# Second layer's first weight group prepared on GpSimd during the first layer's attention

## The chip, the cores and the metric
The kernel runs on one core of a Trainium2 chip. The metric is the time of one execution on the device in microseconds (us), as the median of several runs. The engines are called as in the profile: PE is TensorE's matmuls and PEld its weight loads, DVE is VectorE, ACT is ScalarE, POOL is GpSimd, SP is SyncE. SPq, ACTq and POOLq are the places from which those three issue DMAs.

## What is computed
One inference step of a hybrid encoder with two layers. It runs over a prompt of 2048 tokens and a sample of 32 tokens that share the weights of width 1024. Layer 0 mixes a pooling branch with sliding-window attention; layer 1 is forgetting attention with 16 heads. Each layer is a norm, one combined input projection, a mixer, a gate and an output projection:

```python
def fox_layer(x, k_prefix, v_prefix, logf_prefix, norm_g, w_in, b_forget, qn_g, kn_g, w_out):
    h = rms_norm(x, norm_g)
    proj = h @ w_in
    q, k, v, gate, fpre = jnp.split(proj, [MIX_C, 2 * MIX_C, 3 * MIX_C, 4 * MIX_C], axis=-1)
    ...
    return x + (attn * jax.nn.silu(gate)) @ w_out, k, v, logf
```

All inputs are float32. The kernel gets float32 precision from cheaper matmuls by writing each operand as a sum of two parts, hi (a rounded copy) and lo (the rest), and adding three products: hi with hi, hi with lo, lo with hi.

## The kernel before
The program is one long list of instructions without loops at run time. A planner in the compiler sets the order of the instructions on every engine ahead of the run: where an engine would stand idle by its reckoning, a later instruction that is ready there is put in. During the run each engine, and each queue that issues DMAs, works its list strictly in that order and waits at the head of it.

The stages around the change are these.

- **Layer 0's input projection** (lines 339 to 556) holds the transposed, normalized tokens in `h0` to `h5` of pool `ah`, 16,384 to 24,576 bytes a partition each, with two weight tiles `whl` of 16,384 bytes (pool `aw`) that its column groups use in turn.
- **Layer 0's attention and output projection** (lines 594 to 747) runs in 21 steps over 17 tiles, first the sample and then the 16 tiles of the prompt. A tile goes through five stages, one step each: `stage_load` (L623 to L629: `kk`, `v2` and `qs`, issued from POOL), `stage_scores` (L653 to L665), `stage_values` (L671 to L704, with the gate's product L703 and the split of `mp` on POOL), `stage_out` (L710, and L577 in `out_proj`) and `stage_norm` (L718 to L728). The norm takes its root in `rstd_bits`: L142 to L145 on DVE, then three Newton steps of four small instructions each (L147 to L150) on POOL; then L720 on DVE scales the tile to `hn`, L725 transposes it on PE, L726 copies it out on ACT to `hT`, and L728 stores it to `h1T`. The output weights `wo0` to `wo7` are loaded at step 2 (L564, four of the loads from POOL, four from SP) through the four buffers `xr` and split on ACT and DVE.
- **Layer 1's input projection** (lines 752 to 886) takes `h` back from `h1T` in `load` (L223 into three buffers `hst`, then ACT's cast and DVE's subtraction, L155 and L158 in `split`), and the weights in 16 groups of 256 columns in `weights` (L239 loads 128 rows, L242 scales them by the norm's gains, L155 or L157 and L158 split them into hi and lo). Each group has eight such steps, k = 0 to 7. The first group is prepared by `prefetch` with `fast=True`, on DVE and ACT; every later one on POOL while the group before it is multiplied (L271, or L296 where tokens are the columns). Two tiles `whl` take turns, and three small buffers `wst` take the loads.

SBUF pools are stacked: on the left from the bottom up, on the right from the top down, in the order in which the code opens them. A pool that opens takes the ground of pools that have been closed. An instruction that writes a tile there waits for the last users of the tiles that lay on the same bytes.

Of the kernel before, what the change touches and what calls it, by code (L numbers as in the profile page):

```python
# [17 lines left out]
P = 128  # L18
# [16 lines left out]
CW = 256  # L35
# [7 lines left out]
def hybrid_step_kernel(ctx: ExitStack, tc: tile.TileContext, *args):  # L43
# [93 lines left out]
    def rstd_bits(ss, np_, count):  # L137
        """as rstd_of, for one column and without a table: a first guess from the exponent's bits, then Newton"""
        v = small.tile([P, 1], F32, name="bv", tag="bv")[:np_]
        r = small.tile([P, 1], F32, name="br", tag="br")[:np_]  # L140
        t = small.tile([P, 1], F32, name="bt", tag="bt")[:np_]
        nc.vector.tensor_scalar(out=v, in0=ss, scalar1=1.0 / count, scalar2=EPS, op0=ALU.mult, op1=ALU.add)  # L142
        iv, ir = v.bitcast(I32), r.bitcast(I32)
        nc.vector.tensor_scalar(out=ir, in0=iv, scalar1=1, scalar2=None, op0=ALU.logical_shift_right)
        nc.vector.tensor_scalar(out=ir, in0=ir, scalar1=-1.0, scalar2=float(0x5F3759DF), op0=ALU.mult, op1=ALU.add)  # L145
        for _ in range(3):
            nc.gpsimd.tensor_tensor(out=t, in0=r, in1=r, op=ALU.mult)  # L147
            nc.gpsimd.tensor_tensor(out=t, in0=t, in1=v, op=ALU.mult)
            nc.gpsimd.tensor_scalar(out=t, in0=t, scalar1=-0.5, scalar2=1.5, op0=ALU.mult, op1=ALU.add)
            nc.gpsimd.tensor_tensor(out=r, in0=r, in1=t, op=ALU.mult)  # L150
        return r
# [13 lines left out]
    def flush(n=0):  # L165
        """issue the stores that wait, but for the last n"""
        while len(pending) > n:
            dst, src, eng = pending.pop(0)
            eng.dma_start(dst, src)

    # ------------------------------------------------------------------
    # one layer's input projection, h^T held as exact hi/lo parts
    # ------------------------------------------------------------------
    class Proj:
        def __init__(self, es, w, g, tagp, cw, side):
# [8 lines left out]
            self.wp = es.enter_context(pool_of(name=tagp + "w", bufs=2))  # L184
# [3 lines left out]
        def at(self, which, tok, n):  # L188
            """hi (0) or lo (1) part of h^T for tokens [tok, tok + n): [P, KT, n]"""
# [41 lines left out]
        def weights(self, cols, fast=False):  # L231
            width = sum(n for _, n in cols)
            hl = self.wp.tile([P, 2, KT, self.cw], F32R, name="whl", tag="whl")
            hi, lo = (hl[:, i, :, :width] for i in range(2))
            for k in range(KT):
                st = self.wp.tile([P, self.cw], F32, name="wst", tag="wst", bufs=3)[:, :width]
                at = 0
                for c0, n in cols:
                    nc.sync.dma_start(st[:, at:at + n], self.w[k * P:(k + 1) * P, c0:c0 + n])  # L239
                    at += n  # L240
                eng = nc.vector if fast else nc.gpsimd
                eng.tensor_scalar_mul(st, st, self.g[:, k:k + 1])  # L242
                if fast:
                    split(hi[:, k], lo[:, k], st, nc.scalar, nc.vector)
                else:
                    split(hi[:, k], lo[:, k], st, nc.gpsimd, nc.gpsimd)
            return hi, lo

        def prefetch(self, plan, fast=False):
            """the column groups in the order of use; the next one's weights are loaded ahead"""  # L250
            self.plan = [list(c) for c in plan]
            self.ahead = self.weights(self.plan.pop(0), fast)
# [47 lines left out]
        def turns(self, new=None):  # L300
            """the turn that waits, one step behind the arithmetic it needs"""
# [4 lines left out]
        def head_norm(self, src, np_, nh, gB, eng):  # L306
            """src: [np, nh, 64] (PSUM or SBUF) -> normalized, scaled tile [np, nh, 64]"""
# [13 lines left out]
    def turn(pt, ev, o, t0, h0, npair, dstT):  # L321
        """normalized heads [P, 2 token tiles, npair x 2 heads x 64] -> exact hi / lo parts, transposed"""
# [11 lines left out]
    # ------------------------------------------------------------------  # L334
    # layer 0, input projection and pooling mixer
    # ------------------------------------------------------------------
    smp_es = ExitStack()

    with ExitStack() as es:
# [91 lines left out]
        # ALiBi with the chunk mask, keys = 128 before the tile and its own 128  # L431
# [11 lines left out]
        # the sample's keys, values and queries for the sliding window, hi / lo parts  # L443
# [114 lines left out]
    # ------------------------------------------------------------------  # L558
    # output projection weights, as exact hi/lo parts
    # ------------------------------------------------------------------  # L560
# [6 lines left out]
    def out_proj(pp, pool, lhs, wo, xres, dst, n, eng):  # L567
        """lhs: for 128 tokens (hi, lo) APs [P, KT, 128]; for the sample one AP [P, KT, 64]"""
# [22 lines left out]
    # ------------------------------------------------------------------  # L591
    # layer 0, sliding-window attention and output projection
    # ------------------------------------------------------------------
    with ExitStack() as es:
# [18 lines left out]
        def stage_load(t):  # L613
# [4 lines left out]
            if t < NT:  # L618
# [7 lines left out]
                v2[t] = ld.tile([P, 2, P], F32R, name="v2", tag="v2", bufs=5)  # L626
# [118 lines left out]
        for n in range(NT + 1 + 4):  # L745
            with tc.high_priority(offset=300) if n < 3 else nullcontext():
                step(n)

    # ------------------------------------------------------------------
    # layer 1, input projection  # L750
    # ------------------------------------------------------------------
    late = ctx.enter_context(pool_of(name="late", bufs=1))
    mhs = late.tile([P, KT, 2 * NS], F32R, name="mhs", tag="mhs")
    with ExitStack() as es:
        pj = Proj(es, w_in1, g1c, "c", CW + 16, "right")
# [10 lines left out]
                    + [[(b + c * CW, CW)] for b in (0, 1024, 3072) for c in range(4)], fast=True)  # L766
# [26 lines left out]
        # log forget gates and their running sums  # L793
        with pool_of(name="lf", bufs=1) as lf:
# [28 lines left out]
            def running_sums(src_h, nt, dst, tag):  # L823
                """src_h: [P, 16, nt] with positions t*128+p; dst: DRAM [16*nt, 128]"""
# [63 lines left out]
        # forgetting attention of the sample group, one pair of heads  # L888
# [11 lines left out]
        def sample_pair(hp):  # L900
            """generator: both heads side by side, the queries block diagonal"""
# [70 lines left out]
        for gc in range(4):  # L972
            if gc:
                whi, wlo = pj.next_weights()
            for tch in range(NTC):
                for cc in range(2):
# [3 lines left out]
                    # twice the gate, x * (1 + tanh(x / 2)); the half comes in with the softmax's sums  # L980
# [20 lines left out]
    # ------------------------------------------------------------------  # L1001
    # layer 1, forgetting attention over the prompt
    # ------------------------------------------------------------------
    with ExitStack() as es:
# [9 lines left out]
        def load_head(h, half):  # L1014
            """one head's operands for half of the tokens"""
# [16 lines left out]
        def scores(h, qb, sm, prs):  # L1032
            """generator: one q block's probabilities, in steps"""
# [27 lines left out]
        def values(h, I, prs, dst, a, o):  # L1061
            """generator: one q group's weighted values, transposed, into dst[a]"""
# [53 lines left out]
        def weave(main, n_main, side, n_side):  # L1116
            """side steps spread evenly among the main steps"""
# [66 lines left out]
        # layer 1, output projection  # L1184
# [24 lines left out]
        def halves(t):  # L1209
            """one token tile's mixed values as hi / lo parts"""  # L1210
# [45 lines left out]
```

## Time and profile before
| | us |
|---|---|
| median of 3 runs | 2679.44 |
| lowest and highest | 2678.52, 2679.57 |
| span of the profiled execution, from the first to the last instruction | 2675.6 |

The profile shows one execution on the chip. Its span is 3.8 us below the median of the runs; the rest lies ahead of the first and behind the last instruction. Times of the trace are counted from the start of the span. Matmuls are pipelined, so a busy TensorE is not one at its peak.

### The profile page before, as it was taken

The numbers are of one execution on the slowest core, as the hardware profiler recorded it, in microseconds if no ns is written. First come the engines' busy times: TensorE is split into PE (matmuls) and PEld (weight loads), VectorE is DVE, ScalarE is ACT, GpSimd is POOL, SyncE is SP. The second block draws the span as 40 slices with busy tenths as digits, with TensorE's granted clock in tenths as the row PEclk, the third lists the DMA queues.
The fourth block names the chain that finished last, engine by engine and source line by source line (L and its number), as shares of the span: only waits on it lengthen the run. The fifth ranks groups of instructions, "written<-read, shape, count | busy, mean of one in ns | idle before, by whom it ended". The sixth has DMA issues, their size and how long they took to land. (4 is left out here: it accounts for less than half of the span.)

```text
span 2675.6 us, 47345 instructions
## 1 busy us (share of the span) xinstructions
PE 2586.7 (97%) x17259; PEld 2345.5 (88%) x17259; DVE 1604.6 (60%) x3847; ACT 1166.4 (44%) x2424; POOL 1149.9 (43%) x1583
## 2 busy tenths in 40 slices
PE   6999999799998999999999999999999999999999
PEld 6999999688887999999999998887888878877787
DVE  7650244778765115554553324889988988888521
ACT  5321111556554122222222114777777777777310
POOL 4454240455534434554554422555555555553100
PEclk9999999799998999999999999999999999999999
DMA  6342110976738443445555316544354455443642
GB/s 187 101 110 88 44 47 23 211 185 169 181 100 266 161 159 97 105 111 132 144 146 139 94 62 162 145 113 122 97 148 120 102 120 141 111 103 90 194 149 75
DMA packets 314120, 338.14 MB, mean 126 GB/s; under 512 B 32311, under 2 KB 263887, under 8 KB 313886
## 3 DMA queue, kind: packets, MB, share of 16 engines
q1 hardware_dynamic: 233550, 242.82, 31.6%
q0 software_dynamic: 76320, 87.98, 15.1%
q10 hardware_dynamic: 4016, 4.31, 0.5%
q8 instruction: 136, 2.23, 0.4%
q14 instruction: 98, 0.80, 0.1%
HBM read 203.05 MB, written 132.06 MB: 125 GB/s over the span
## 5 line engine op out<-in xcount | busy, mean ns | idle before, releaser
L271 PE MATMUL pm<-whl,h 128*128 128x256 f32 (+1 forms) x5760 | 713.7, 283 | 6.3 <-ACT h L155 3.1
L271 PEld LDWEIGHTS pm<-whl,h 128*128 128x128 f32 x5760 | 694.9, 190 | 7.9 <-ACT h L155 3.5
L296 PE MATMUL pm<-h,whl 128*128 128x384 f32 (+2 forms) x2880 | 472.3, 322 | 0.0
L296 PEld LDWEIGHTS pm<-h,whl 128*128 128x128 f32 x2880 | 455.3, 188 | 1.8
L158 POOL TENSOR_TENSOR pl<-pf,ph 128x512 fp32r<-128x512 f32 (+3 forms) x270 | 303.6, 1127 | 263.5 <-DVE ph L157 253.2
L1058 ACT ACTIVATE pr<-pr,mnf 128x128 f32<-128x128 f32 (+15 forms) x256 | 309.6, 1211 | 61.6 <-DVE mnf L1053 60.6
L1077 PE MATMUL pt<-ident,pr 128*128 128x128 f32 x2176 | 323.3, 274 | 5.5 <-DVE pl L158 5.4
L1077 PEld LDWEIGHTS pt<-ident,pr 128*128 128x128 f32 x2176 | 251.2, 141 | 39.3 <-DVE pl L158 11.4
L158 DVE TENSOR_TENSOR pl<-pt,ph 128x512 fp32r<-128x512 f32 (+3 forms) x436 | 261.4, 612 | 39.8 <-ACT ph L155 36.7
L1048 PE MATMUL ps<-ka,qs 128*128 128x512 f32 (+3 forms) x640 | 253.6, 397 | 16.9 <-DVE mnf L1053 15.9
L1053 DVE CUSTOM_DVE_ANT_0 pr<-ps,cb 128x1024 f32<-128x1024 f32 (+7 forms) x256 | 248.8, 981 | 17.9 <-PE ps L1049 9.2
L155 ACT CAST ph<-pt 128x512 fp32r<-128x512 f32 (+3 forms) x436 | 224.9, 529 | 60.9 <-PE pt L1077 44.0
L1070 PE MATMUL pa<-pl,vhl 128*128 128x512 f32 (+3 forms) x640 | 249.2, 395 | 2.3 <-POOL pl L158 2.3
L1070 PE MATMUL pa<-ph,vhl 128*128 128x512 f32 (+3 forms) x640 | 243.6, 383 | 3.8 <-DVE ph L157 3.2
L1049 PE MATMUL ps<-kb,qs 128*128 128x512 f32 (+3 forms) x640 | 228.8, 366 | 0.0
L1082 ACT COPY pf<-pt 128x512 f32<-128x512 f32 (+3 forms) x270 | 140.3, 523 | 66.9 <-PE pt L1077 63.9
L157 DVE CAST ph<-pf 128x512 fp32r<-128x512 f32 (+3 forms) x270 | 143.9, 537 | 35.8 <-ACT pf L1082 35.7
L577 PE MATMUL po<-wo,mh 128*128 128x512 f32 x512 | 162.9, 398 | 0.8 <-ACT mh L155 0.5
L1048 PEld LDWEIGHTS ps<-ka,qs 128*128 128x128 f32 x640 | 121.2, 189 | 46.5 <-DVE mnf L1053 30.3
L157 POOL CAST whl<-wst 128x256 fp32r<-128x256 f32 (+1 forms) x184 | 73.3, 420 | 186.3 <-PE pm L281 105.5
L242 POOL TENSOR_SCALAR wst<-wst,g1c 128x256 f32<-128x256 f32 (+1 forms) x120 | 115.5, 968 | 88.2 <-DMA wst<-in_w_in_dram 86.4
L311 DVE TENSOR_REDUCE ssh<-sq 128x8 f32<-128x512 f32 (+3 forms) x99 | 62.4, 630 | 137.3 <-ACT sq L309 137.2
(396 smaller groups left out, 4050.9 us busy)
## 6 DMA issues: line engine op xcount, KB each, us to landing
qT<-qhl SPq DMA_DIRECT2D x192, 128.0 KB, 2.4
qs<-qT POOLq DMA_DIRECT2D x48, 512.0 KB, 7.3
wst<-in_w_in_dram SPq DMA_DIRECT2D x168, 128.0 KB, 2.6
kT<-qhl SPq DMA_DIRECT2D x128, 128.0 KB, 2.4
ka<-kT POOLq DMA_DIRECT2D x32, 512.0 KB, 7.1
kb<-kT POOLq DMA_DIRECT2D x64, 256.0 KB, 9.0
cb<-cT SPq DMA_DIRECT2D x32, 512.0 KB, 9.6
vhl<-vH POOLq DMA_DIRECT2D x32, 512.0 KB, 4.7
```

The source lines that it names most:

```text
L155: nc.scalar.copy(hi, src)
L157: eng_hi.tensor_copy(hi, src)
L158: eng_lo.tensor_tensor(out=lo, in0=src, in1=f32(hi), op=ALU.subtract)
L271: nc.tensor.matmul(ps[:, j, :], a[:, kt, :], b[:, kt, :], start=(i == 0), stop=(i == 3 * KT - 1))
L296: nc.tensor.matmul(ps, a[:, kt, c:c + P], b[:, kt, :], start=(i == 0), stop=(i == 3 * KT - 1))
L577: nc.tensor.matmul(ps, a[:, kt, :], wo[kt][:, b, cs], start=(i == 0), stop=(i == 3 * KT - 1))
L1048: nc.tensor.matmul(ps[:, s0:s0 + m], lhs, ka[:, ks], start=True, stop=False)
L1049: nc.tensor.matmul(ps[:, s0:s0 + m], lhs, kb[:, ks], start=False, stop=not diag)
L1053: nc.vector.tensor_tensor_reduce(out=pr[:, c0:c0 + n], in0=ps[:, :n], in1=cb[:, :n], scale=1.0, scalar=mns[-1][:, 0:1] if mns else 3e38, o ...
L1058: nc.scalar.activation(pr[:, :L], pr[:, :L], AF.Exp, bias=mns[-1][:, 0:1], scale=-1.0, accum_out=sm)
L1070: nc.tensor.matmul(pa[:, r0 * P:], vhl[b], pp[:, r0:].rearrange("p r q -> p (r q)"), start=(b == 0 and i == 0), stop=(b == nkb - 1 and i = ...
L1077: nc.tensor.transpose(pt[:, r, :], prs[r][:, b * P:(b + 1) * P], ident)
```

## The change
`weights` is cut out of the class `Proj` into a function `weight_steps` that gives the group's tiles and a generator of its eight steps. A pool `cw` is opened ahead of layer 0's attention and stays open into layer 1. At step 8 of the attention's loop the first group's tile is made in it, and from there on each step of the loop asks for one step of the group, all of it on GpSimd. `Proj` of layer 1 gets this pool as its `wp`: the three `wst` buffers lie there for good, and the `whl` tiles of the groups alternate between two homes of one buffer each, that pool and one of its own. The first group is handed to `prefetch` ready-made. In the attention `v2` has four buffers in place of five. The small pool `late` goes to the right side. Comments and docstrings are dropped as well.

```diff
+    def weight_steps(wp, cw, w, g, cols, fast, home=None):
+        width = sum(n for _, n in cols)
+        hl = (home or wp).tile([P, 2, KT, cw], F32R, name="whl", tag="whl", bufs=1 if home else 2)
+        hi, lo = (hl[:, i, :, :width] for i in range(2))
+
+        def steps():
+            for k in range(KT):
+                st = wp.tile([P, cw], F32, name="wst", tag="wst", bufs=3)[:, :width]
+                at = 0
+                for c0, n in cols:
+                    nc.sync.dma_start(st[:, at:at + n], w[k * P:(k + 1) * P, c0:c0 + n])
+                    at += n
+                (nc.vector if fast else nc.gpsimd).tensor_scalar_mul(st, st, g[:, k:k + 1])
+                if fast:
+                    split(hi[:, k], lo[:, k], st, nc.scalar, nc.vector)
+                else:
+                    split(hi[:, k], lo[:, k], st, nc.gpsimd, nc.gpsimd)
+                yield
+
+        return hi, lo, steps()
...
-            self.wp = es.enter_context(pool_of(name=tagp + "w", bufs=2))
+            own = es.enter_context(pool_of(name=tagp + "w", bufs=2))
+            self.wp = wp or own
+
+            self.homes = [wp, own] if wp else None
...
         def weights(self, cols, fast=False):
...
+            if self.homes:
+                self.homes.reverse()
+            hi, lo, steps = weight_steps(self.wp, self.cw, self.w, self.g, cols, fast, self.homes and self.homes[0])
+            for _ in steps:
+                pass
             return hi, lo
...
-            self.ahead = self.weights(self.plan.pop(0), fast)
+            cols = self.plan.pop(0)
+            self.ahead = first or self.weights(cols, fast)
...
+    cw_es = ctx.enter_context(ExitStack())
+    c_wp = cw_es.enter_context(pool_of(name="cw", bufs=2))
...
-                v2[t] = ld.tile([P, 2, P], F32R, name="v2", tag="v2", bufs=5)
+                v2[t] = ld.tile([P, 2, P], F32R, name="v2", tag="v2", bufs=4)
...
         for n in range(NT + 1 + 4):
+            if n == 8:
+                *c_first, c_steps = weight_steps(c_wp, CW + 16, w_in1, g1c, [(2048, CW)], False, c_wp)
+            if n >= 8:
+                next(c_steps, None)
...
-    late = ctx.enter_context(pool_of(name="late", bufs=1))
+    late = ctx.enter_context(pool_of(name="late", bufs=1, side="right"))
...
-        pj = Proj(es, w_in1, g1c, "c", CW + 16, "right")
+        es.enter_context(cw_es)
+        pj = Proj(es, w_in1, g1c, "c", CW + 16, "right", c_wp)
...
-                    + [[(b + c * CW, CW)] for b in (0, 1024, 3072) for c in range(4)], fast=True)
+                    + [[(b + c * CW, CW)] for b in (0, 1024, 3072) for c in range(4)], first=tuple(c_first))
```

## Rows read from the trace of the kernel before

**Rows 1.** TensorE's busy tenths in 40 equal slices of the span, from the page.
```profile
PE   6999999799998999999999999999999999999999
```

**Rows 2.** Busy time of each engine in windows at the seam, granted clock, DMA.
```profile
805.00:810.00 5.00, 0.05 (x1) 0.00 (x0) 2.25 (x9) 2.91 (x7) 1.38 (x7) 0.80 0.89 258
810.00:815.00 5.00, 1.94 (x8) 1.57 (x8) 1.77 (x4) 1.17 (x2) 1.09 (x6) 0.50 0.83 260
815.00:820.00 5.00, 0.80 (x2) 0.50 (x2) 2.01 (x6) 4.38 (x8) 0.00 (x0) 0.50 0.64 184
820.00:825.00 5.00, 4.07 (x19) 4.07 (x20) 4.76 (x5) 0.42 (x2) 4.25 (x3) 0.50 0.58 162
```

**Rows 3.** Timeline of the seam: start, duration, engine, line, operation, idle before and releaser.
```profile
807.16 0.15 DVE L144 TENSOR_SCALAR br<-bv 128x1 int32<-128x1 int32 x1
...
807.56 0.42 DVE L158 TENSOR_TENSOR whl<-wst,whl 128x256 fp32r<-128x256 f32 x1 [0.25 <-ACT whl L155]
807.90 0.15 DVE L145 TENSOR_SCALAR br<-br 128x1 int32<-128x1 int32 x1
...
811.53 0.75 DVE L720 TENSOR_SCALAR hn<-xr,br 128x1024 f32<-128x1024 f32 x1 [2.00 <-POOL br L150]
...
812.43 1.94 PE L725 MATMUL pt<-ident,hn 128*128 128x128 f32 x8 [7.38 <-DVE hn L720]
...
814.41 0.58 ACT L726 COPY hT<-pt 128x512 f32<-128x512 f32 x1 [0.22 <-PE pt L725]
...
815.45 1.02 ACT L155 CAST whl<-wst 128x256 fp32r<-128x256 f32 x3 [0.45 <-ACT hT L726]
...
816.37 2.93 ACT L155 CAST h<-hst 128x1024 fp32r<-128x1024 f32 x3
...
817.46 0.80 PE L271 MATMUL pm<-whl,h 128*128 128x256 f32 x2 [3.09 <-ACT h L155]
...
819.66 3.69 DVE L158 TENSOR_TENSOR h<-hst,h 128x1024 fp32r<-128x1024 f32 x3
...
820.93 11.33 PE L271 MATMUL pm<-whl,h 128*128 128x256 f32 x78 [2.67 <-DVE h L158]
```

**Rows 4.** The tile `hst`: its loads (ns min/median/max) and their time to landing.
```profile
L223 SPq DMA_DIRECT2D hst<-h1T x17: 359/408/1417, 802.2 to 855.1; - x17
...
DMA to landing us min/median/max: 3.7/5.2/7.0
```

**Rows 5.** The tile `wst`: POOL's three operations of a step, ns min/median/max.
```profile
L242 POOL TENSOR_SCALAR wst<-wst,g1c x27: 918/926/2638, 820.1 to 942.9; 128x256 f32<-128x256 f32 x19, 128x272 f32<-128x272 f32 x8
L157 POOL CAST whl<-wst x24: 391/402/1391, 822.8 to 939.3; 128x256 fp32r<-128x256 f32 x16, 128x272 fp32r<-128x272 f32 x8
L158 POOL TENSOR_TENSOR whl<-wst,whl x24: 726/742/1530, 823.7 to 939.8; 128x256 fp32r<-128x256 f32 x16, 128x272 fp32r<-128x272 f32 x8
```

**Rows 6.** Timeline at the last values of the attention, TensorE.
```profile
794.25 0.39 PE L695 MATMUL pa<-pl,v 128*128 128x512 f32 x1
```

**Rows 7.** Timeline of POOL: first and last operations of the third group's preparation.
```profile
870.35 1.09 POOL L157 CAST whl<-wst 128x256 fp32r<-128x256 f32 x3 [7.13 <-PE pm L281]
...
892.77 0.74 POOL L158 TENSOR_TENSOR whl<-wst,whl 128x256 fp32r<-128x256 f32 x1
```

**Rows 8.** Timeline of POOL inside the Newton steps of one tile.
```profile
717.22 0.79 POOL L623 DMA_DIRECT2D kk<-kT  x1 [0.27 <-issue]
...
719.22 0.22 POOL L149 TENSOR_SCALAR bt<-bt 128x1 f32<-128x1 f32 x1
```

**Rows 9.** Timeline of POOL at the start of the attention.
```profile
480.20 2.21 POOL L564 DMA_DIRECT2D xr<-in_w_out_dram  x4 [79.69 <-PE pm L538]
```

**Rows 10.** Busy time in a window at the attention's start (PE, PEld, DVE, ACT, POOL).
```profile
486.00:491.00 5.00, 0.78 (x4) 0.36 (x4) 4.65 (x12) 4.98 (x19) 2.24 (x5) 0.50 1.32 339
```

**Rows 11.** What ACT waited for, 480 to 510 us: total, times, longest.
```profile
ACT wo L155 <- DMA xr<-in_w_out_dram: 7.6, 4, 2.7
```

**Rows 12.** Line L665 of DVE in the attention, ns min/median/max.
```profile
L665 DVE TENSOR_SCALAR pr<-pr,sm x128: 273/345/1865, 509.4 to 778.5; 128x256 f32<-128x256 f32 x120, 128x128 f32<-128x128 f32 x8
```

More of the change, by code (lines that the diff above doesn't have):

```diff
@@ L169, in flush, with __init__ @@
             eng.dma_start(dst, src)
+    def weight_steps(wp, cw, w, g, cols, fast, home=None):
[16 more added lines that the diff above has]
+        return hi, lo, steps()
     class Proj:
-        def __init__(self, es, w, g, tagp, cw, side):
+        def __init__(self, es, w, g, tagp, cw, side, wp=None):
             self.w = w
@@ L231, in weights, with prefetch @@
         def weights(self, cols, fast=False):
[L232 to L246, printed above, removed]
+            if self.homes:
[3 more added lines that the diff above has]
+                pass
             return hi, lo
-        def prefetch(self, plan, fast=False):
+        def prefetch(self, plan, fast=False, first=None):
             self.plan = [list(c) for c in plan]
-            self.ahead = self.weights(self.plan.pop(0), fast)
+            cols = self.plan.pop(0)
+            self.ahead = first or self.weights(cols, fast)
         def next_weights(self):
```

## The prediction
> **What bounds the kernel now.** I read the page first: in its 40 slices TensorE reads 9 or more nearly everywhere [rows 1], so only the stretches in which it stands still can give time back. Behind the first slice there are two worth reading: the eighth (468 to 535 us, a 7), the start of layer 0's attention, and the thirteenth (803 to 870 us, an 8), the seam between the layers. The change speaks of the seam, so I read that next, in windows of 5 us: from 805 to 825 us TensorE is busy for 0.05, 1.94, 0.80 and 4.07 us, at a granted clock that falls to 0.50 [rows 2], which is 1.2 of 2.4 GHz. Then the order of events there [rows 3]. TensorE waits 7.38 us for `hn`, the normalized last tile, then 3.09 us for the first cast of `h`, then 2.67 us for the first `lo` of `h`: 13.1 us. The slow clock after the pause adds half of the 1.94 + 0.80 + 4.07 us of work done at it, 3.4 us. So the seam costs about 16.5 us, and that is the most that the change can win there.
>
> What ends last at the seam is the point. Only the last two waits touch the weights. The longest one, 7.38 us, is the normalization of tile 15: DVE computes the first guess, POOL runs twelve small Newton steps, DVE scales (811.53), TensorE transposes, ACT copies (814.41). Weight work holds that chain up once: the `lo` of a weight (807.56, 0.42 us) sits between L144 (807.16) and L145 (807.90) on DVE [rows 3]. And the first `h` cast stands on ACT at 816.37, behind the copy of tile 15 and three weight casts, although its `hst` was asked for at 802.2 and loads land in 3.7 to 7.0 us [rows 3, 4]. So neither its data nor the weights held it for most of that time, but its place in ACT's queue. I read this as the planner's rule: the first writer into the pool of `h` is put behind the last users of the closed pools on whose ground that pool lies. `hT`, `hn` and `xr` of the attention lie there before and after the change alike.
>
> **The change part by part.** *Removed at the seam:* eight steps of scale, cast and subtraction on DVE and ACT, and their eight loads on SP. On the chain this frees two pieces. Between the end of L144 (807.31) and L145 stand 0.59 us, of which I count 0.55. After the copy of tile 15 the three casts of 815.45 to 816.37 go: 0.92 us. The first `h` cast then runs from about 814.9 to 815.95, its `lo` (a third of 3.69, 1.23 us) follows at once to 817.2, and the third matmul of L271, which needs it, starts at about 817.25 instead of 820.93 [rows 3]. That is 3.7 us; the 7.38 us wait and the slow clock stay.
>
> *Added on GpSimd:* 8 steps of L242 (0.926), L157 (0.402) and L158 (0.742) [rows 5], 16.6 us of POOL, with 8 loads on SP. Their ground is free once layer 0's projection is through, their place in the code is low in priority, and the planner fills idle places, so I expect most of them early in the attention, around 485 to 540 us. There they lie beside a TensorE that waits for other things. The cover is thin where POOL's own chain is TensorE's: the mix of L703, the Newton steps, and the issues of the next tiles' loads, all in one queue. A step of at most 0.93 us can stand ahead of each.
>
> *Moved without being named:* the second group. Before, it starts after the first. Now its home is a place of its own on the ground of `kk` and `v2`, free when the last values are read, at 794.64 [rows 6]. How such a group runs is shown by the third: six casts and subtractions at once from 870.35, then at the pace of its loads to 893.5 [rows 7], 23 us. Put at 794.64 it runs to about 818, exactly over the Newton chains of tiles 14 and 15. And the queue does let other work into such a chain: at 717.22 the issues for a later tile stand between two Newton steps, and L149 comes at 719.22, some 2 us late [rows 8]. What is left of the second group there is 3 x (0.402 + 0.742) + 5 x 2.07 = 13.8 us. With two Newton chains (3.5 each, from the end of L145 to L720 [rows 3]) POOL has 20.8 us to do from 794.64, which ends at 815.4 where tile 15's chain ends at 811.5 now. So tile 15 comes between 0 and 3.9 us later; I take 3, since the ready steps fill nearly every gap. Seam: -3.7 + 3 = -0.7 us, bounds -3.7 and +0.2.
>
> *The ground shifts.* The home is 17,408 + 3,264 bytes a partition, `v2` gives back 1,024, so every tile of the attention lies 19,648 bytes higher. Before, the first output weights wait in POOL's queue until 480.20, 79.69 us, for TensorE [rows 9]: by the sizes in the code, `xr` lies on the weight tile that layer 0's last group reads to its end. Higher up, three of four `xr` lie on the other weight tile, which is free by then, and `kk` of the first tiles on ground free since about 445. So some of the loads that crowd 480 to 515 (339 GB/s, and TensorE busy for 0.78 of 5 us at half clock [rows 10]) can run before it. ACT waits 7.6 us there for these loads [rows 11]: the bound of the gain. Against it, the order of that start is planned anew, and DVE (4.65 of 5 us busy [rows 10]) is close to the bound itself, so I take -2 us; the other end, +4, is half of what ACT waits there now, for a worse order.
>
> *The attention itself.* POOL's 16.6 us fall beside DVE. L665 takes 345 ns at the median and 1865 at most [rows 12]: some of its runs are held. I take +1 us for all holds on the way to TensorE, with ends 0 and +3. The Trainium skill (SBUF — State Buffer, Who interferes with whom) has it that VectorE in a two-port mode and GpSimd lock each other out of a shared pair for a whole instruction. The spread of L665 agrees; by that rule taken at its hardest (each of the 24 instructions holds a DVE one for its length, and all of it reaches TensorE) the sum would be 16.6 us worse, where the median says most are not held. `v2` with 4 buffers in place of 5 still leaves its loads some two tiles of lead; I cost it at nothing, and if that lead fails, each miss is one landing of a few us.
>
> **Sum.** -0.7 - 2 + 1 = -1.7 us against the profiled span of 2675.6; the 3.8 us between that and the median of 2679.44 lie around the span and stay. So 2677.7, rounded 2677.5.
>
> **Rivals.** *Restart at once:* L271 goes ahead of tile 15's transposes because its weights are long there. The 16.5 us go and 2663 is left. For it: the seam's size, and 802.2 for `hst`. Against it: the place of the `h` casts behind the copy, which weights don't explain [rows 3, 4]. 6%.
>
> *The start gains:* the shifted ground lets loads run under layer 0's projection; all 7.6 us of ACT's wait go, and the seam gives some 1.5: 2670. For it: a wait of 79.69 us that hangs on an address [rows 9]. Against it: DVE's share. 23%.
>
> *Slower, POOL's queue:* a scale step waits in POOL's queue for its load, in a stretch in which loads land late, and behind it wait the tiles' loads, the mix and the Newton steps. In the trace of before a wait of this kind stands with later groups, where nobody else needs POOL. It decides against the change from the point where tile loads lose their lead or two or three tiles' mixes come late. I price it at three such stalls of 2 us (as the one in [rows 8]), with the seam's +0.2 and the attention's +1: about +7, 2686.5. 21%.
>
> That the change does nothing (the steps come at the end of the attention after all) would give 2679 and lies within the forecast.
>
> **How the numbers follow.** About 0.2%, 5.4 us, is what a measurement of this kernel can tell from no change. The forecast with 50% is a time within that of before; its own range is 2674 to 2684. Faster: 6 + 23 = 29%. Slower: 21%. The low end takes in the start's gain with both bounds, -3.7 - 7.6, so 2668; the high end adds +0.2, +4 and +3, so 2687. Outside are the restart at once and the worst of POOL's queue.
>
> **What would show it.** Right: no L242 or `whl` work on DVE or ACT between 796 and 824; POOL's L242 in the first third of the attention; TensorE still waits for `hn` at the seam, for 6 to 11 us at half clock afterwards; the `h` casts follow the copy of tile 15 directly; L157 and L158 of the second group on POOL between 795 and 818, some between Newton steps. The first `xr` and `kk` loads before 470. Wrong: L271 ahead of the last L725; a seam without a pause; POOL waits in the attention that reach TensorE; a start that isn't shorter by any microsecond.

## The result, and the profile after

| | before | after |
|---|---|---|
| median, us | 2678.98 (2677.03 to 2679.57, 4 runs) | 2706.36 (2705.34 to 2707.78, 4 runs) |
| span of the profiled execution | 2675.6 | 2703.9 |

The change makes the kernel 1.1% slower: the ratio is 1.0107, with a 95% interval from 1.0095 to 1.0119 (the two medians alone give 1.0102). In after's trace the lines have other numbers: L577 is L593, L564 is L580, L242 is L187, L271 is L287, L703 is L721, L720 is L738, L725 is L743.

The page's line of TensorE's busy tenths in 40 slices, which answers [rows 1], has the loss in the ninth and the thirteenth slice:

```profile
PE   6999999789997999999999999999999999999999
```

To see how much of it lies where, I cut the trace at three marks: the end of the last matmul of layer 0's projection, the end of the last output matmul of layer 0, and the first L271 or L287 behind which they run on without a pause. What lies between the first two I call the attention, and between the last two the seam. The views of windows of before and of after between these marks (columns as in [rows 2]: TensorE's busy time is the second number, the granted clock the third from the end):

```profile
481.98:804.17 322.19, 303.19 (x1586) 250.01 (x1585) 246.55 (x714) 183.15 (x512) 152.64 (x326) 0.95 0.71 174
804.17:820.93 16.76, 3.62 (x19) 2.71 (x16) 7.75 (x21) 8.96 (x17) 3.31 (x13) 0.61 0.76 226
```

```profile
484.12:826.47 342.35, 315.53 (x1584) 255.95 (x1584) 236.23 (x716) 182.38 (x513) 165.21 (x342) 0.93 0.60 157
826.47:850.55 24.08, 4.68 (x19) 3.64 (x18) 3.94 (x8) 5.74 (x9) 12.58 (x34) 0.56 0.53 158
```

The attention is 20.2 us longer, the seam 7.3. Layer 0's projection ends 2.1 us later (in the traces below it ends up to 3.8 us later than in before, in kernels too that don't touch it, so I count from its end), and 1.3 us are made good afterwards: 28.3 in all. Of the attention's 20.2 us, TensorE stands still for 7.8 more (26.8 in the place of 19.0) and is busy for 12.3 more with the same matmuls, at a mean clock of 0.93 in the place of 0.95.

The seam, which answers [rows 2] and [rows 3], first on TensorE and then on POOL in the timeline of after:

```profile
833.86 1.94 PE L743 MATMUL pt<-ident,hn 128*128 128x128 f32 x8 [7.39 <-DVE hn L738]
845.18 1.94 PE L743 MATMUL pt<-ident,hn 128*128 128x128 f32 x8 [9.38 <-DVE hn L738]
849.29 0.80 PE L287 MATMUL pm<-whl,h 128*128 128x256 f32 x2 [2.17 <-ACT h L155]
...
820.67 0.20 POOL L147 TENSOR_TENSOR bt<-br 128x1 f32<-128x1 f32 x1
820.81 1.20 POOL L158 TENSOR_TENSOR whl<-wst,whl 128x256 fp32r<-128x256 f32 x1
822.60 0.93 POOL L187 TENSOR_SCALAR wst<-wst,g1c 128x256 f32<-128x256 f32 x1 [0.59 <-DMA wst<-in_w_in_dram]
823.50 0.19 POOL L148 TENSOR_TENSOR bt<-bt,bv 128x1 f32<-128x1 f32 x1
823.67 0.92 POOL L187 TENSOR_SCALAR wst<-wst,g1c 128x256 f32<-128x256 f32 x1
824.54 0.39 POOL L157 CAST whl<-wst 128x256 fp32r<-128x256 f32 x1
824.91 0.19 POOL L149 TENSOR_SCALAR bt<-bt 128x1 f32<-128x1 f32 x1
```

Where TensorE waited once for `hn` (7.38 us), it now waits twice, for tile 14 and for tile 15, 16.8 us together. Between the Newton steps of tile 14 (L147 to L150) stand the second group's scales, casts and subtractions. The twelve steps, some 3.3 us by themselves, take from 820.67 to 832.93.

The first group's steps run on POOL from 496 to 571 us, in the attention's start. A stretch of POOL's timeline in after, behind it the two lines of before that it is read against:

```profile
511.66 2.11 POOL L157 CAST whl<-wst 128x256 fp32r<-128x256 f32 x3
519.10 0.78 POOL L641 DMA_DIRECT2D kk<-kT  x1 [5.33 <-PE ps L672]
519.87 1.21 POOL L643 DMA_DIRECT2D kk<-kT  x2
521.04 0.93 POOL L647 DMA_DIRECT2D qs<-qT  x1
521.96 2.24 POOL L158 TENSOR_TENSOR whl<-wst,whl 128x256 fp32r<-128x256 f32 x3
531.42 0.61 POOL L157 CAST mh<-mp 128x512 fp32r<-128x512 f32 x1 [7.22 <-DMA mp<-m0T]
...
537.69 1.83 POOL L187 TENSOR_SCALAR wst<-wst,g1c 128x256 f32<-128x256 f32 x2 [1.69 <-DMA wst<-in_w_in_dram]
539.49 1.28 POOL L158 TENSOR_TENSOR ml<-mp,mh 128x512 fp32r<-128x512 f32 x1
...
563.69 1.83 POOL L187 TENSOR_SCALAR wst<-wst,g1c 128x256 f32<-128x256 f32 x2 [7.70 <-DMA wst<-in_w_in_dram]
```

```profile
523.63 1.29 POOL L158 TENSOR_TENSOR ml<-mp,mh 128x512 fp32r<-128x512 f32 x1
...
535.17 0.78 POOL L623 DMA_DIRECT2D kk<-kT  x1 [0.35 <-PE ps L654]
```

`ml` of the first prompt tile (the low half that its output projection reads) is ready at 540.8 us; in before it is ready at 524.9. POOL also stands for 7.70 us at a scale for its load, in the middle of the sample's Newton steps. That looks like my rival of POOL's queue. The 7.22 us for the load of `mp` are another matter: in the run below that only shifts the ground, without weight steps in the attention, such a wait is there too (8.4 us at most), in the one with the weight steps alone it is not (0.3). The runs had to tell whether it is the wait, POOL's time, or the shifted ground.

### The profile page after: what moved, and what is told of

The parts are those of the page before. It is cut to its first block, busy times and chain, and to the rows that moved or that the text cites. A ratio compares the mean times of both kernels' runs of the same rounds, so it can differ in the third digit from the quotient of the medians.

```text
span 2703.9 us, 47347 instructions
## 1 busy us (share of the span) xinstructions
PE 2600.6 (96%) x17259; PEld 2352.6 (87%) x17259; DVE 1591.5 (59%) x3831; ACT 1162.1 (43%) x2416; POOL 1154.8 (43%) x1607
## 3 DMA queue, kind: packets, MB, share of 16 engines
q0 software_dynamic: 76320, 87.98, 14.8%
## 5 line engine op out<-in xcount | busy, mean ns | idle before, releaser
L287 PE MATMUL pm<-whl,h 128*128 128x256 f32 (+1 forms) x5760 | 713.9, 284 | 3.2 <-ACT h L155 2.2
L287 PEld LDWEIGHTS pm<-whl,h 128*128 128x128 f32 x5760 | 695.0, 189 | 5.0 <-ACT h L155 2.6
L1071 PE MATMUL ps<-ka,qs 128*128 128x512 f32 (+3 forms) x640 | 253.5, 396 | 16.3 <-DVE mnf L1076 15.5
L593 PE MATMUL po<-wo,mh 128*128 128x512 f32 x512 | 161.5, 398 | 4.2 <-DVE xr L604 3.5
L187 POOL TENSOR_SCALAR wst<-wst,g1c 128x256 f32<-128x256 f32 (+1 forms) x128 | 118.1, 929 | 81.5 <-DMA wst<-in_w_in_dram 81.0
```

The source lines that it names most:

```text
L287: nc.tensor.matmul(ps[:, j, :], a[:, kt, :], b[:, kt, :], start=(i == 0), stop=(i == 3 * KT - 1))
L1071: nc.tensor.matmul(ps[:, s0:s0 + m], lhs, ka[:, ks], start=True, stop=False)
```

## The experiments

Three theories. For the attention: *G*, the shifted ground made a worse order, and *P*, POOL's queue (later split into *W*, waits for loads, and *O*, POOL's time and the places of the steps). For the seam: *S*, the second group between the Newton steps. All the runs stand in one table. "Ratio" is to the kernel before, with its interval; "idle" is TensorE's standing time in the attention; "2nd ml" is when `ml` of the second prompt tile is done on POOL. Except for the ratio all are us of the profiled run, the last counted from the attention's start.

| kernel | ratio | attention | idle | 2nd ml | seam |
|---|---|---|---|---|---|
| before | 1 | 322.2 | 19.0 | 48.4 | 16.8 |
| after | 1.0107 (1.0095 to 1.0119) | 342.4 | 26.8 | 71.7 | 24.1 |
| ground | 1.0019 (1.0010 to 1.0029) | 330.7 | 18.9 | 53.2 | 15.9 |
| steps | 1.0102 (1.0087 to 1.0118) | 345.3 | 30.9 | 72.4 | 16.7 |
| a_wx | 1.0122 (1.0107 to 1.0137) | 339.2 | 27.6 | 71.1 | 27.5 |
| a_nlast | 1.0085 (1.0068 to 1.0102) | 346.9 | 29.2 | 72.3 | 11.5 |
| steps_noload | 1.0107 (1.0093 to 1.0121) | 350.9 | 33.3 | 80.0 | 16.6 |
| steps_nott | 1.0102 (1.0088 to 1.0116) | 348.5 | 32.7 | 72.9 | 16.8 |
| steps_fast | 1.0028 (1.0016 to 1.0040) | 326.6 | 21.8 | 47.9 | 16.6 |
| v2only | 1.0005 (0.9996 to 1.0014) | 321.3 | 20.3 | 50.5 | 16.6 |
| ground_wx | 1.0075 (1.0060 to 1.0091) | 327.4 | 22.3 | 53.2 | 29.5 |
| a_paced | 1.0090 (1.0075 to 1.0106) | 341.9 | 25.8 | 58.9 | 20.2 |
| a_paced_nlast | 1.0072 (1.0059 to 1.0085) | 344.0 | 27.8 | 58.5 | 12.4 |
| a_pf_nlast | 1.0058 (1.0044 to 1.0072) | 339.7 | 24.1 | 58.7 | 13.3 |
| a_best | 1.0035 (1.0022 to 1.0047) | 333.5 | 23.9 | 54.5 | 12.7 |
| b_nlast | 1.0001 (0.9992 to 1.0009) | 322.0 | 18.9 | 47.4 | 16.3 |
| b_dram | 1.0030 (1.0020 to 1.0041) | 321.7 | 18.3 | 47.6 | 20.0 |
| b_dram_nlast | 1.0008 (0.9999 to 1.0016) | 321.8 | 18.1 | 47.0 | 14.8 |

### One part alone

`ground`, on the kernel before:

```diff
+        gnd = es.enter_context(pool_of(name="cw", bufs=1))
+        gt = gnd.tile([P, 5168], F32, name="gnd", tag="gnd")
+        nc.gpsimd.memset(gt[:, 0:1], 0.0)
...
-                v2[t] = ld.tile([P, 2, P], F32R, name="v2", tag="v2", bufs=5)
+                v2[t] = ld.tile([P, 2, P], F32R, name="v2", tag="v2", bufs=4)
```

> The kernel before with the ground of the change alone: 20,672 B a partition are taken ahead of the attention's tiles (nothing is prepared in them) and v2 gives back a buffer; the first weight group is prepared where the kernel before prepares it, at the seam. In the changed kernel the last output matmul before the seam ends at 826.5 us, in the kernel before at 804.2, 22.3 later. Theory G (the ground): the shifted tiles make the planner put the output weights' loads and casts behind the first tiles' scores, and that is what the attention lost, so this kernel is 18 to 22 us slower than before: 2697 to 2701, with the first output matmul of the sample 10 to 15 us later than 514.7 and the seam's pause as before (16.8 us from the last output matmul to the first unbroken L271). Theory P (POOL's queue): the loss comes from the weight steps in POOL's queue, of which this kernel has none in the attention: 2675 to 2681.

`steps`, on the kernel before, with `v2` as above and a pool `cz` (`wz`) opened above all others of the attention:

```diff
+            if n >= 8 and n < 8 + KT:
+                k = n - 8
+                if k == 0:
+                    hl = wz.tile([P, 2, KT, CW + 16], F32R, name="whl", tag="whl", bufs=1)
+                st = wz.tile([P, CW + 16], F32, name="wst", tag="wst", bufs=3)[:, :CW]
+                nc.sync.dma_start(st, w_in1[k * P:(k + 1) * P, 2048:2048 + CW])
+                nc.gpsimd.tensor_scalar_mul(st, st, g1c[:, k:k + 1])
+                split(hl[:, 0, k, :CW], hl[:, 1, k, :CW], st, nc.gpsimd, nc.gpsimd)
```

> The kernel before with the weight steps alone: the 24 POOL operations and 8 loads of the first group are issued in the attention as in the change, into a home above all of the attention's tiles, so that those move by no more than the 1,024 B that v2 gives back; nobody reads what they prepare, and the group is prepared once more at the seam as before. Theory G: 2677 to 2682, nothing lost but the extra POOL work. Theory P: POOL waits for weight loads in front of tile loads and Newton steps, 2697 to 2701, with POOL waiting 5 us or more for wst in the sample's Newton chain.

`ground` is 0.19% slower and `steps` 1.02%. The steps alone, with the seam as it was, cost what the whole change costs, so P is right for most of it; the ground's part is real but smaller, 8.5 us of the attention in the profiled run and about 5 us in the time. `v2only` (`bufs=4` and nothing else) says that this part isn't the buffer:

> The kernel before with four v2 buffers in the place of five, and nothing else; this is the part that the run with the ground alone and the run with the steps alone have in common, and it moves the pools above v2 by 1,024 B. If the shift of 20,672 B is what made the run with the ground alone 8.5 us longer in the attention, this one stays within 2 us of the kernel before: 2675 to 2681. If the missing buffer is, it is 2683 to 2687.

It is as fast as before. The two parts don't add: 8.5 and 23.1 alone, 20.2 together.

`a_wx`, on the changed kernel, tried to mend the ground:

```diff
+        wx = es.enter_context(pool_of(name="b5", bufs=4))
         bp = es.enter_context(pool_of(name="b1", bufs=1))
...
-        wx = es.enter_context(pool_of(name="b5", bufs=4))
```

> The changed kernel with one line moved: the pool of the xr buffers (through which the output weights are loaded) is opened ahead of that of the output weights, so that it lies on ground that comes free earlier. All weight steps stay. Theory G: the output weights are prepared in time again and the start's gain (6.8 us more TensorE work from 450 to 500 us) is kept: 15 to 22 us of the attention's 22.3 come back, 2684 to 2691; the seam keeps its 24 us. Theory P: nothing comes back, 2703 to 2708.

Nothing came back in time: the attention is 3.2 us shorter, the seam 3.4 longer. The sample's output projection starts at 518.8 us where after starts it at 526.5 and before at 514.8, but the first prompt tile's starts at 540.8, as late as in after (541.3; before 523.6). Its `ml` isn't the reason, for here it is done at 535.4. TensorE's last long wait ahead of it is for DVE, whose eight L683 (L665 in before, 345 ns each at the median [rows 12]) take 5.82 us while POOL scales weights and makes `ml`:

```profile
531.30 2.80 POOL L187 TENSOR_SCALAR wst<-wst,g1c 128x256 f32<-128x256 f32 x3
...
532.00 5.82 DVE L683 TENSOR_SCALAR pr<-pr,sm 128x256 f32<-128x256 f32 x8
...
534.07 1.28 POOL L158 TENSOR_TENSOR ml<-mp,mh 128x512 fp32r<-128x512 f32 x1
...
539.17 0.58 PE L671 MATMUL ps<-kk,qs 128*128 128x256 f32 x1 [5.87 <-DVE mn L673]
```

### Waits, or POOL's time and place

`steps_noload`, on `steps`:

```diff
-                nc.sync.dma_start(st, w_in1[k * P:(k + 1) * P, 2048:2048 + CW])
-                nc.gpsimd.tensor_scalar_mul(st, st, g1c[:, k:k + 1])
+                nc.gpsimd.tensor_scalar_mul(st, bias[:, 0, :], g1c[:, k:k + 1])
```

> The kernel of the run before that added the weight steps alone, without their eight loads: the scale steps read a table that already stands in SBUF, so the 24 POOL operations stay and nothing in them waits for a transfer (what they prepare is no weight, and nobody reads it). Theory W (waits): what the steps cost is POOL standing at scale steps for their loads (in that run 6.7 us for wst between 480 and 580 us) with tile loads, halves and Newton steps behind: 2680 to 2686. Theory O (place and work): POOL is already busy for 7 of 10 us at the attention's start, and 16.6 us of added work ahead of the tiles' ml halves and of the sample's Newton steps is the loss, with or without loads: 2695 to 2703.

Without a load to wait for it is no faster (1.0107), and its second `ml` is later still. W falls, and with it the mechanism that I had given the rival. What the trace of `steps` shows of POOL is another order:

```profile
522.91 2.14 POOL L158 TENSOR_TENSOR whl<-wst,whl 128x256 fp32r<-128x256 f32 x3
525.00 0.60 POOL L157 CAST mh<-mp 128x512 fp32r<-128x512 f32 x1
526.00 1.39 POOL L587 TENSOR_TENSOR xr<-xr,pos 32x512 f32<-32x512 f32 x1 [0.41 <-ACT pos L586]
527.44 2.77 POOL L753 TENSOR_SCALAR wst<-wst,g1c 128x256 f32<-128x256 f32 x3
536.79 0.80 POOL L624 DMA_DIRECT2D kk<-kT  x1 [6.58 <-PE ps L655]
537.58 0.62 POOL L626 DMA_DIRECT2D kk<-kT  x1
538.20 1.30 POOL L158 TENSOR_TENSOR ml<-mp,mh 128x512 fp32r<-128x512 f32 x1
```

With weight steps in the list, `ml` comes to stand behind another tile's load, and that load waits 6.58 us for TensorE. In before `ml` runs at 523.63, ahead of that load. The tile's output projection comes late too, at 541.88 for 523.61 in before. But `ml` isn't what TensorE waited for last: it was done at 539.50, and the wait just ahead of the projection is one of 0.80 us for DVE's `mn`. TensorE's longest waits from 480 to 600 us, in total, number and longest, two of before and four of `steps`:

```profile
PE ps L653 <- DVE mn L655: 7.2, 4, 3.6
PE pt L690 <- DVE pr L665: 4.0, 1, 4.0
...
PE ps L654 <- DVE mn L656: 10.7, 10, 2.9
PE pt L691 <- DVE pr L666: 4.6, 4, 3.8
PE pa L696 <- DVE pl L158: 3.5, 5, 1.8
PE pa L695 <- ACT ph L155: 3.3, 4, 2.4
```

None of them names POOL, in either trace. How POOL's added work gets into them, these rows don't show.

`steps_fast` takes the same steps from POOL:

```diff
-                nc.gpsimd.tensor_scalar_mul(st, st, g1c[:, k:k + 1])
-                split(hl[:, 0, k, :CW], hl[:, 1, k, :CW], st, nc.gpsimd, nc.gpsimd)
+                nc.vector.tensor_scalar_mul(st, st, g1c[:, k:k + 1])
+                split(hl[:, 0, k, :CW], hl[:, 1, k, :CW], st, nc.scalar, nc.vector)
```

> The run with the weight steps alone once more, its 24 operations taken from POOL: scale and low part on DVE, the high part on ACT, at the same place in the code; loads and home stay, and nobody reads the result. Theory O (POOL's time at the attention's start): the ml halves, mixes and Newton steps come early again, and 15 us or more of the 23.1 come back: 2680 to 2688. Rival D: any work added there delays the first tiles, since DVE is as busy as POOL (16 of 20 us from 480 to 540): 2695 to 2705.

The ratio falls from 1.0102 to 1.0028, the attention from 345.3 to 326.6 us, and the second `ml` is back at 47.9. So most of the loss comes from the work being on POOL, though TensorE's waits name DVE and ACT.

Or was it DVE, held up beside POOL? `steps_nott` puts two casts in the place of each subtraction:

```diff
-                split(hl[:, 0, k, :CW], hl[:, 1, k, :CW], st, nc.gpsimd, nc.gpsimd)
+                for i in (0, 1, 1):
+                    nc.gpsimd.tensor_copy(hl[:, i, k, :CW], st)
```

> The run with the weight steps alone once more, each subtraction on POOL (0.74 us) replaced by two casts (0.40 us each), so that POOL's time and the steps' places stay while the eight two-operand operations are gone (what they leave is no low part, and nobody reads it). Theory O (place and time on POOL): nothing comes back, 2700 to 2706. Rival L: the operations stop DVE while they run (one 128x8 DVE operation took 4.13 us beside a mix and three whl subtractions on POOL, where it takes 0.17), and that is the loss: 2680 to 2690.

Nothing comes back (1.0102), though the longest stop of DVE (L661, 128x8, 4.13 us in `steps`, ending 0.03 us behind POOL's three subtractions) has gone to 0.95. The run doesn't take all holds away, for scales and casts stay: L666 takes 542 ns on average up to 600 us, and 490 in `steps`. What speaks against the holds as a sum is that DVE is busy no longer than before in the attention, 245.8 us in `steps` and 236.2 in after for 246.6, and L665 in it 43.9 and 41.8 us for 49.0 (its 120 operations of 128x256). The Trainium skill (SBUF — State Buffer, Who interferes with whom) has it that a VectorE instruction with two inputs in SBUF is held by a GpSimd one that reads SBUF. L661 agrees, and the holds are there; their sum is not the loss. That single ones lie on TensorE's way, as the eight L683 of `a_wx` do, no run separates from the order.

### The seam

`a_nlast`, on the changed kernel, gives the twelve Newton steps of tiles 14 and 15 to DVE:

```diff
-            r = rstd_bits(ss, n, D)
+            r = rstd_bits(ss, n, D, nc.vector if NT - 2 <= o.t < NT else nc.gpsimd)
```

(`rstd_bits` uses this engine in its loop.)

> The changed kernel with the 12 Newton steps of prompt tiles 14 and 15 on DVE in the place of POOL. Theory S (seam): the second group's weight steps between the Newton steps of the last two tiles make the seam 24.1 us long in the place of 16.8 (from the last output matmul's end to the first unbroken L287), so this kernel gets 7 us or more back: 2696 to 2700, and hn of tile 15 comes less than 7 us after the last output matmul. Rival: the seam is set by the h1T transfers and the casts of h, as long as before whoever does the Newton steps: 2704 to 2708.

The seam falls from 24.1 to 11.5 us, the time to 1.0085; part of the 12.6 us went on an attention 4.6 us longer. S holds. The same edit on the kernel before, `b_nlast`, where nothing stands between these steps:

> The control: the kernel before with the Newton steps of tiles 14 and 15 on DVE. At its seam POOL runs nothing between those steps (12 steps in 3.3 us), so theory S leaves only the steps' own duration to gain: 1 to 2 us, 2675 to 2677. If DVE's Newton steps are by themselves what the seam wants, 5 us or more: 2672 or less.

It changes nothing. So DVE's steps aren't better in themselves; what helps is that nothing can get between them.

`ground_wx` showed S once more where I hadn't looked for it. It is `ground` with `a_wx`'s edit, and has none of the change's weight steps:

> The run with the ground alone once more (20,672 B taken ahead of the attention's tiles, nothing prepared in them), with the pool of the xr buffers opened ahead of that of the output weights, so that the output weights' loads no longer need ground that comes free late. If the 8.5 us that the ground cost in the attention are the output weights' late preparation, they come back, and what is left of the earlier start is a gain: 2671 to 2678. If they are the other tiles' order, it stays at 2681 to 2684.

Neither: the attention gives back 3.2 of its 8.5 us (so by this run the output weights' late loads are less than half of the ground's cost), but the time is 1.0075, by a seam of 29.5 us. Its timeline, in which the second group starts earlier than in before:

```profile
816.07 0.19 POOL L147 TENSOR_TENSOR bt<-br 128x1 f32<-128x1 f32 x1
816.64 0.92 POOL L242 TENSOR_SCALAR wst<-wst,g1c 128x256 f32<-128x256 f32 x1 [0.39 <-DMA wst<-in_w_in_dram]
817.54 0.19 POOL L148 TENSOR_TENSOR bt<-bt,bv 128x1 f32<-128x1 f32 x1
...
834.01 0.19 POOL L150 TENSOR_TENSOR br<-br,bt 128x1 f32<-128x1 f32 x1
...
835.13 1.94 PE L728 MATMUL pt<-ident,hn 128*128 128x128 f32 x8 [23.05 <-DVE hn L723]
```

Here the last tile's Newton steps alone take 18.1 us, and TensorE waits 23.05 us for them.

### Other places for the work

`a_paced`, on the changed kernel, ties each step to its tile by a copy of one column ahead of the step's load; `a_paced_nlast` has `a_nlast`'s edit as well:

```diff
                 st = wp.tile([P, cw], F32, name="wst", tag="wst", bufs=3)[:, :width]
+                if gate:
+                    gate(st)
...
-                *c_first, c_steps = weight_steps(c_wp, CW + 16, w_in1, g1c, [(2048, CW)], False, c_wp)
+                *c_first, c_steps = weight_steps(c_wp, CW + 16, w_in1, g1c, [(2048, CW)], False, c_wp, lambda st: nc.vector.tensor_copy(
+                    st[:, 0:1], tl[order[n - 4]].xr[:, 0:1]))
```

> The changed kernel with each weight step tied to the tile beside which it stands in the code: one DVE copy of a column from that tile's residual into the wst buffer ahead of its load, so that step k can't begin before tile 3 + k has its output projection. All 24 POOL operations and the 8 loads stay, at 620 to 770 us in the place of 496 to 572. Theory E (early): the steps cost only where the attention starts, since later there are no waits on POOL for TensorE to feel: 15 to 20 of the 22.3 us come back, the seam keeps its 24, 2686 to 2692. Theory A (anywhere): the steps delay halves and Newton steps of whichever tile they stand beside, 2700 to 2708.

> Both: the steps tied to their tiles, and the Newton steps of tiles 14 and 15 on DVE. If the start's loss and the seam's loss are two separate things, their gains add: 2706 less 17 less 8, 2678 to 2684, against 2677 for the kernel before, so no better than it but for what the weight work gave at the seam (up to 3.7 us: then 2674). If they are one thing seen twice, 2688 or more.

Neither the start nor the sum is mended: 1.0090 and 1.0072. `a_paced`'s attention is 341.9 us, 11.3 longer than `ground`'s: it is 4.1 us behind at the fourth output projection, before the first tied step on POOL (608.0), and 11.3 at the end of the last. `a_pf_nlast` has the tied steps on DVE and ACT (`fast` true), and `a_best` that and `a_wx`'s edit:

> The changed kernel with the steps of the first group tied to their tiles and the last Newton steps on DVE, as before, and the first group's steps on DVE and ACT in the place of POOL. The run with them on POOL was 2699.5. If POOL's time is what they cost beside the tiles, the 11 us between its attention (344.0) and that with the ground alone (330.7) come back, 2686 to 2691; if any engine's time costs it, 2697 to 2701.

> That, and the xr pool opened ahead of that of the output weights: the change's plan (home, first group ready before the seam) with each of the three losses taken away. If they are the three causes, the attention is as long as before (322 us) and the seam 12 in the place of 16.8: 2671 to 2677, which would beat both kernels. If the ground's loss doesn't go with the xr pool: 2683 to 2690.

`a_pf_nlast` (1.0058) lies between what either theory said: 4.3 us of the attention were POOL's, 9.0 over `ground` were not. `a_best` (1.0035) has the short seam, and 11.3 us too many in the attention. So three causes taken away don't bring back the order that before has.

`b_dram` leaves the attention's ground and order alone. At the third column group of the pooling branch:

```diff
+            for k in range(KT) if g == 2 else ():
+                ks = slice(k * P, (k + 1) * P)
+                st = pj.wp.tile([P, CW], F32, name="wst", tag="wst", bufs=3)
+                nc.sync.dma_start(st, w_in1[ks, 2048:2048 + CW])
+                nc.gpsimd.tensor_scalar_mul(st, st, g1c[:, k:k + 1])
+                wh = pw.tile([P, CW], F32R, name="wh", tag="wh")
+                split(wh, st.bitcast(F32R), st, nc.gpsimd, nc.gpsimd)
+                nc.sync.dma_start(wd[0, ks, :], f32(wh))
+                nc.sync.dma_start(wd[1, ks, :], st)
...
+            for i in range(2):
+                nc.gpsimd.dma_start(self.ahead[i], first[i].rearrange("(k p) c -> p k c", p=P))
```

> The kernel before with the first group's weights prepared on POOL while layer 0's last column groups run, in the 79.7 us in which POOL does nothing, and put by in DRAM as high and low parts; at the seam two transfers bring them into their home, in the place of eight loads and 24 operations on DVE and ACT. Attention's ground and order stay. Theory O: POOL's idle stretch is the place that costs nothing, the attention is as long as before (322 us), and the seam loses the weight work: up to 3.7 us off, 2675 to 2679. Rival: the transfers (2.1 MB where 1.05 MB were loaded) collide with the h loads at the seam: 2681 to 2686.

> The same, with the Newton steps of tiles 14 and 15 on DVE. With the weights in DRAM the second group's steps can go on POOL early, as in the change; if they get between the last Newton steps again, the run without this edit keeps or lengthens the 16.8 us of the seam and this one has 12 us, as the changed kernel had with the same edit (11.5): 2671 to 2676. If the seam's length is that of the h chain alone, both runs are alike.

POOL's 24 steps at 401 to 432 us cost the attention nothing (321.7 and 321.8 us). But `b_dram` is 0.30% slower, some 8 us. Its seam of 20.0 us, 3.2 longer, is the part of it that the trace explains, and there the rival was right in kind. DMA issues of `b_dram` from 800 to 826 us (number, KB each, median us to landing), and then ACT's timeline there:

```profile
whl<-wd POOLq DMA_DIRECT2D x2, 1024.0 KB, 13.7
...
h1T<-hT SPq DMA_DIRECT2D x1, 512.0 KB, 14.2
```

```profile
822.01 1.07 ACT L744 COPY hT<-pt 128x512 f32<-128x512 f32 x2 [13.37 <-DMA h1T<-hT]
```

The store of tile 14's `hT` takes 14.2 us beside the two transfers where it takes 4.2 in before, and `hT` has one buffer, so the copy of tile 15 waits 13.37 us for it. With the Newton steps on DVE the transfers start at 799.8 in the place of 804.5, the store takes 6.2 us, the seam is 14.8, and the time is that of before (1.0008, interval 0.9999 to 1.0016). None of the kernels beats it.

## Why the prediction was wrong

**The seam's first step was right.** No weight work is left on DVE and ACT there, the first cast of `h` follows the copy of tile 15 directly (847.16 and 848.19 on ACT), and TensorE doesn't start at once: *restart at once* didn't come. Without the second group in the way the seam would have been won: 11.5 us in `a_nlast` for 16.8. Right too: `v2`'s missing buffer costs nothing that can be measured (`v2only`).

**The term of the second group was mis-sized.** Its place was right (POOL, from 817 us, between the Newton steps of tiles 14 and 15). I took 3 us from adding up POOL's work, with 3.9 as the most. The seam got 7.3 us longer, although the two waits behind `hn` had become 3.1 us shorter (2.17 and 0.46 for 3.09 and 2.67, where I had 3.7): so the second group cost some 10 us. The sum was the wrong model. The twelve steps depend on one another, so each hole between them takes in a weight step, and each weight step can wait for its load: in after 12.3 us for tile 14's steps, in `ground_wx` 18.1 for tile 15's.

**The term of POOL in the attention failed as a step.** I wrote that the 16.6 us fall "beside a TensorE that waits for other things" and took +1, 0 to 3. [rows 12] answered for DVE's holds and not for POOL's own chain, which I named and didn't price in the sum. `steps` gives the price, 23.1 us of attention, and `steps_fast` gives 18.7 of them back. TensorE did wait for other things there, for DVE and ACT. But these were no cover: POOL, DVE and ACT were all some 7 of 10 us busy from 480 to 490, and with POOL's work beside them the same waits got longer. By which way, `ml` and the loads that come later or single holds of DVE, stays open.

**The rival of POOL's queue had the right sign and the wrong mechanism and size.** It said scale steps waiting for loads, 7 us. The waits are there (7.70 us once), but `steps_noload` loses as much without them.

**The ground's term had the wrong sign.** Loads did run earlier: the first `kk` at 448.42 and the first `xr` at 465.48 us, and TensorE works 6.8 us more from 450 to 500. The gain was given back at once: in `ground` alone the attention is 8.5 us longer, beyond my worse end of +4, although TensorE idles no longer (18.9 us); it is the work that takes longer, 311.7 us busy for 303.2. An estimate, busy time weighted with the granted clock in windows of 2.5 us, puts 4.2 of these 8.5 us down to the slow clock, and 7.2 of after's 12.3; the rest stays open. In after, what TensorE does from 485 to 530 us comes in pieces, at a mean clock of 0.59 (0.67 in before, where it waits first and runs nearly without a break from 510 on). `ground` has 0.67 there as well and loses later, with 0.88 from 520 to 540 and 0.91 from 580 to 600, where before has 1.00.

**What stays open.** Why tied steps on DVE and ACT still cost some 9 us over `ground`, and which difference in order makes `ground`'s 8.5. Over all eighteen rows of the table the attention is by groups the longer the later the second `ml` is (47 to 51 us: 321 to 327; 53 to 59: 327 to 344; 71 to 80: 339 to 351). That is a parallel: `steps_fast` shows POOL's added work as a cause, and no run shows `ml` as the way to TensorE.

## What to carry to other kernels

Idle time of an engine counts by stretch, and the engine that a wait names need not be the one without room: TensorE's waits named DVE and ACT, and the same work cost 23.1 us of attention on POOL and 4.4 on those two. Before work is put beside a stretch that waits, try it on more than one engine. A chain of small dependent steps on an engine in whose list a planner fills gaps is as long as whatever fits between them; if it ends a stage, put it where nothing else is ready. And a tile that moves in SBUF is an edit of the whole order: `ground` computes nothing new and changes the time by 0.19%, `ground_wx` by 0.75%, so test the layout alone before crediting or blaming the work that came with it.

## What the runs showed of the hardware that I had not expected

A small transfer can take long to land beside big ones of another queue: the 512 KB store of `hT` took 14.2 us beside two transfers of 1 MB each that were issued 3.2 us earlier, 6.2 where they were issued 10.7 us earlier, and 4.2 without them. And the granted clock makes a start in pieces dearer (the estimate above: 7.2 us in after). In before TensorE is at full speed from 515 us to 600. In after the clock has come back at 505 (0.99 in a window of 5 us), and behind pauses it falls again, to 0.50 at 515, 0.78 at 550 and 0.51 at 580.
